# Storing the two halves of the latent heads' value product apart, and adding them when the outputs are loaded again

## The chip, the cores and the metric

The kernel runs on one core of one Trainium2 chip, in one launch. The metric is the device time of that launch in microseconds, as the median of repeated executions; less is better. Before the change the median of three executions is 1318.42 us (1316.21 to 1319.64). The core has five engines with an instruction queue each: TensorE (PE, with its weight loads as PEld), VectorE (DVE), ScalarE (ACT), GpSimd (POOL) and SyncE (SP). In this kernel SP issues every transfer, and the 16 DMA engines carry them out.

## What is computed

One layer of a streaming encoder on a sequence of 1024 tokens with 1024 channels, all in float32: a modulated norm, a mixer with two groups of eight attention heads, one output projection with a gated residual, and a gated MLP with a causal convolution. What matters here is the mixer's first group, the latent heads, and the projection behind both groups:

```
q, k, v from low-rank latents, 8 heads, q and k 96 wide, v 64 wide
o_mla = mla_attention(q, k, v)          # softmax(q k^T / sqrt(96)) v, chunk-causal
o_ca  = chunk_attention(cq, ck, cv, rel_bias[l])     # 8 heads, 9-chunk key band
mixed = jnp.dot(jnp.concatenate([o_mla, o_ca], axis=-1), w_out[l])
x = x + g_a[:, None, :] * mixed
```

The result must keep nearly float32 accuracy. TensorE's fast number formats don't have it in one operand, so the kernel splits operands into a high and a low half (hi, the rounded value, and lo, what is left) and adds the products of the halves. That is why one matrix product here is two or three matmuls.

## The kernel before

**Order of the work.** The kernel is written in a tile framework. Tiles are drawn from pools by tag with a number of buffers, and a tile whose buffer is still in use makes its first writer wait. A planner puts the instructions of each engine in order ahead of time, by priority and by its own forecast of times; each engine then runs its queue strictly in that order, waiting on semaphores. Where the program says issue_after, the planner must keep that order.

**Attention.** The work is cut into units: one head and one half g of the 1024 queries (512 queries). First come 16 units of the band heads, then 16 of the latent heads (two groups of four heads, each with g = 0 and 1). A unit has four tiles of 128 queries. For each tile, TensorE makes the scores (L807), DVE takes the minimum of the negated scores (L826), ACT the exponential with its sum (L833), DVE the reciprocal of the sum (L835, L836), POOL the high half of the scaled probabilities (hi, L73 from L852) and DVE the low half (L855), both in float16. SP then issues a transpose by DMA (L867) of each piece into PT tiles. Three tiles later TensorE multiplies the transposed probabilities by the values (L895). Beside this chain runs other work on the same engines: up-projections for later heads, and the projection of the band heads' outputs into part_d (f_oca, L710).

**The end of a unit.** The stationary operand of L895 is 128 columns wide: the 64 columns of the values' high half and the 64 of their low half. So the product in PSUM, pv, holds two partial results, in partitions 0 to 63 and 64 to 127, for 512 queries. For an even head ACT copies partitions 64 to 127 of pv, scaled, into partitions 0 to 63 of an SBUF tile named om (L904), and DVE scales the other half and adds it to the tile (L905); for an odd head the halves change places. SP stores the 64 rows to oT_d in DRAM (L909), which holds the outputs of all heads, transposed: 8 blocks of 128 rows with two heads each, by 1024 tokens. The om tile has one buffer, and pv has one. The store of the very last unit is held back (the list held, L907) and issued only after the first four loads of the next stage; that unit's tile is from another pool (tag R).

**The output projection.** For each of eight tiles of 128 tokens, o_load (L1066) reads the four latent blocks from oT_d into a tile ol of 128 by 512 (256 KB, in pieces of 512 B, as 128 tokens of a row are contiguous; L1069). ACT makes the high half oh (L77, called from L1070), POOL puts the low half back into ol (L84, from L1071). TensorE then does 24 matmuls of 512 columns for the tile (L1188 by way of L154 to L156), which take the three products hi*hi, hi*lo and lo*hi for four blocks and two column halves. DVE adds part_d's row (L1193), multiplies by the gate gabc (L1194) and adds x (L1195). SP stores the sum (L1196), ACT squares it (L1197), POOL and DVE norm it (L1202), and TensorE transposes it for the MLP (L1096).

The loads for this stage are o_load for tiles 0 to 3, then the held store, then gabc, and for each tile pa from part_d (L1169) and x (L1173, issued after the last of the first four o_loads). The weights of the MLP's first columns, wu, are loaded here as well (L1145), and split by ACT and POOL. ol and oh have four buffers each, so o_load of tile t + 4 follows TensorE's work on tile t.

Of the kernel before, what the change touches and what calls it, by code (L numbers as in the profile page):

```python
# [13 lines left out]
F32 = mybir.dt.float32  # L14
# [4 lines left out]
AF = mybir.ActivationFunctionType  # L19
# [3 lines left out]
MUL, ADD, SUB, MIN, MAX = ALU.mult, ALU.add, ALU.subtract, ALU.min, ALU.max  # L23

P = 128
D = 1024
S = 1024
NT = S // P
ND = D // P
# [35 lines left out]
def layer_kernel(ctx, tc, I, out):  # L65
    nc = tc.nc
    pe, act, dve, pool, sp = nc.tensor, nc.scalar, nc.vector, nc.gpsimd, nc.sync

    def f32(ap):
        return ap.bitcast(F32)  # L70
# [4 lines left out]
    def hi_of(eng, o, i):  # L75
        if eng == "a":
            act.activation(o, i, AF.Copy)  # L77
        elif eng == "p":
            pool.tensor_scalar(o, i, 1.0, 0.0, op0=MUL, op1=ADD)
        else:  # L80
            dve.tensor_copy(o, i)

    def lo_of(eng, o, i, hi):
        (pool if eng == "p" else dve).tensor_tensor(o, i, f32(hi), op=SUB)  # L84

    cst = ctx.enter_context(tc.tile_pool(name="cst", bufs=1))
    dram = ctx.enter_context(tc.tile_pool(name="dram", bufs=1, space=bass.MemoryType.DRAM))
    oT_d = dram.tile([ND, P, S], F32, name="oT_d")
    part_d = dram.tile([NT, P, D], F32, name="part_d")
    ga_d = dram.tile([P, D], F32, name="ga_d")  # L90
    x1_d = dram.tile([NT, P, D], F32, name="x1_d")
# [23 lines left out]
    anchor = {}  # L115
# [22 lines left out]
    def rtile(name, shape=(P, 512), dt=F32):  # L138
        return apg.tile(list(shape), dt, name=name, tag="R", bufs=4)
# [596 lines left out]
    def qk_page(src, name, rows, tag, bufs, gain):  # L736

        pt = page_psum(src, name, rows)
        if gain is None:
            hi, lo = q2(f"{name}h"), q2(f"{name}l")  # L740
            act.activation(hi[:rows], pt[:rows], AF.Copy)
            dve.tensor_tensor(lo[:rows], pt[:rows], f32(hi[:rows]), op=SUB)
            return hi, lo
        pg = at.tile([P, 2, 512], F32R, name=name, tag=tag, bufs=bufs)
        act.activation(pg[:rows, 0], pt[:rows], AF.Copy, scale=gain)
        dve.scalar_tensor_tensor(pg[:rows, 1], pt[:rows], gain, f32(pg[:rows, 0]), op0=MUL, op1=SUB)
        return pg
# [22 lines left out]
    class Unit:  # L770


        def __init__(u, nm, base, rows, pages, vst, g, band, bias, odd, dst_d, vs):
            u.nm, u.base, u.rows, u.pages, u.vst, u.g = nm, base, rows, pages, vst, g
            u.band, u.bias, u.odd, u.dst_d, u.vs = band, bias, odd, dst_d, vs
            u.pt = {}

        def scores(u, i):

# [92 lines left out]
        def values(u, i):  # L872

            if i % 4 == 1:
                u.pv = ps.tile([P, 512], F32, name=f"pv{u.nm}_{u.g}", tag="pv", bufs=1)
            c0 = (i % 4 - 1) * P
            todo = []
            for x in range(2):
                if (i - 1, x) not in u.pt:
                    continue  # L880
                tt, where = u.pt[i - 1, x]
                for j, at_ in where.items():
                    for h in range(2):
                        if len(at_) == 2:
                            b0, b1 = at_[0][h], at_[1][h]
                            todo.append((0, j, c0, 2 * P, tt[:, b0:b1 + 1:b1 - b0, :]))
                        else:
                            todo.append((1, j, c0 + at_[0][2] * P, P, tt[:, at_[0][h], :]))
            todo.sort(key=lambda v: v[0])
            with tc.high_priority(offset=OFF_V):  # L890
                for x, (_, j, c, w, mov) in enumerate(todo):
                    dst = u.pv[:, c:c + w]
                    if w > P:
                        dst = dst.rearrange("p (a b) -> p a b", a=2)
                    last = pe.matmul(dst, u.vst(j), mov, start=(x == 0), stop=(x == len(todo) - 1),  # L895
                                     skip_group_check=True)
                trail.append(last.ins)
                if i % 4 == 3:
                    final = u is units[-1]
                    dst = rtile(f"o{u.nm}_{u.g}") if final else \  # L900
                        at.tile([P, 512], F32, name=f"o{u.nm}_{u.g}", tag="o", bufs=1)
                    r0, r1 = (slice(64, 128), slice(0, 64)) if u.odd else (slice(0, 64), slice(64, 128))
                    inv = vscale[u.vs][1]
                    act.activation(dst[r0], u.pv[r1], AF.Copy, scale=inv[r1])  # L904
                    dve.scalar_tensor_tensor(dst[r0], u.pv[r0], inv[r0], dst[r0], op0=MUL, op1=ADD)  # L905
                    if final:
                        held.append(lambda: sp.dma_start(u.dst_d[r0, u.g * 512:(u.g + 1) * 512], dst[r0]))  # L907
                    else:
                        anchor["om"] = sp.dma_start(u.dst_d[r0, u.g * 512:(u.g + 1) * 512], dst[r0]).ins  # L909
            return 56 * sum(w // P for _, _, _, w, _ in todo)  # L910

    qlow = [at.tile([P, 512], F32R, name=f"qlow{n}") for n in range(3)]
# [6 lines left out]
    held = []  # L919
# [36 lines left out]
    def mla_unit(gr, hh, g):  # L956
        o = hh % 2

        def prep():
            q = qk_page(lambda j: mq[gr, (4 * g + j) // 2][:, j % 2, hh, :], f"mq{gr}{hh}_{g}", QK, "Q", 2, None)  # L960
            k = qk_page(lambda j: mk[gr, (4 * g + j) // 2][:, j % 2, hh, :], f"mk{gr}{hh}_{g}", QK, "K", 3, gk_m[:QK])
            pages[gr, hh, g] = (q, k)
        u = Unit(f"m{gr}{hh}", 0, QK,
                 lambda: (pages[gr, hh, g][0], [pages[gr, hh, i][1] for i in range(g + 1)]),
                 lambda j: mv[gr, j // 2][:, j % 2, hh].rearrange("p a b -> p (a b)"),
                 g, False, None, o, oT_d[2 * gr + hh // 2], ("m", gr))
        u.prep = prep
        u.need = [f"up{gr}"] if g == 0 else ["up1"]
        u.needv = []
        return u  # L970
# [55 lines left out]
    first = [anchor["pe"]]  # L1026
    units = [ca_unit(p, g, o) for p in range(4) for g in range(2) for o in range(2)]
    units += [mla_unit(gr, hh, g) for gr in range(2) for hh in range(4) for g in range(2)]
    ready = []
    tiles = [(u, i) for u in units for i in range(4 * u.g, 4 * u.g + 4)]  # L1030
    for n in range(len(tiles) + DEPTH):
        if n < len(tiles):
            u, i = tiles[n]
# [9 lines left out]
        if n >= DEPTH:  # L1043
            u, i = tiles[n - DEPTH]
# [18 lines left out]
    go = goo.__enter__()  # L1063
    oh, ol, ox = {}, {}, {}

    def o_load(t):  # L1066
        ol[t] = go.tile([P, 4, P], F32R, name=f"ol{t}", tag="ol", bufs=4)
        oh[t] = go.tile([P, 4, P], F32R, name=f"oh{t}", tag="oh", bufs=4)
        anchor["ol"] = sp.dma_start(f32(ol[t][:]), oT_d[0:4, :, t * P:(t + 1) * P].rearrange("k p t -> p k t")).ins  # L1069
        hi_of("a", oh[t][:], f32(ol[t][:]))  # L1070
        lo_of("p", ol[t][:], f32(ol[t][:]), oh[t][:])  # L1071

    for t in range(4):
        o_load(t)
# [569 lines left out]
def build(arrays):  # L1644
    nc = bacc.Bacc("TRN2", target_bir_lowering=False, num_devices=1, dynamic_dma_scratch_size=1024)
    I = {k: nc.dram_tensor(k, v.shape, mybir.dt.from_np(v.dtype), kind="ExternalInput").ap()
         for k, v in arrays.items()}
    out = nc.dram_tensor("out_0_dram", (S, D), F32, kind="ExternalOutput").ap()
    with tile.TileContext(nc, schedule_with_timeline_sim=True) as tc, ExitStack() as ctx:
        layer_kernel(ctx, tc, I, out)  # L1650
    return nc
# [8 lines left out]
```

## Time and profile before

| what | value |
|---|---|
| median of three executions | 1318.42 us |
| the profiled execution | 1320.49 us |
| its span, first to last instruction | 1318.7 us |
| mean granted TensorE clock | 0.964 of full |
| latent units: first and last copy of om on ACT | 399.2 and 599.6 us |
| output projection: first and last matmul of its tiles | 598.8 and 652.4 us |
| transfers issued | 190.83 MB in 223690 packets |
| loads of ol | 8 of 256.0 KB, median 9.3 us to landing |
| loads of x | 8 in this stage of 512.0 KB, median 9.4 us to landing |

The profile is one execution, taken by the hardware profiler. A group's row gives the line of the code, the engine, the operation, the tile written and the tiles read, the shape, how many there were, and min, median and max or the mean of one in ns. A row of the order of time begins with start and length in us; brackets behind it give the idle time of that engine just before and what ended it. A row of waits reads: who, for whom, us in total, times, longest. A row of stretches has the busy us of each engine with the number of instructions, then the granted clock, the share of the DMA engines that was busy, and GB/s. SPq is SP's queue: its rows are the issuing of transfers, and the transfer itself lands later.

### The profile page before, as it was taken

To read this page: it belongs to the slowest core of one execution; us is meant where nothing else is said; L and a number is where in the kernel's file an instruction comes from. 1 tells how busy PE (TensorE), PEld (TensorE's weight loads), DVE (VectorE), ACT (ScalarE), POOL (GpSimd) and SP (SyncE) were. 2 spreads that over 40 slices of the span, in tenths; PEclk is the share of its full clock that TensorE was granted. 3 is DMA by queue.
4 is the path that set the end of the run, shared out by engine and by line. 5 is a ranking of instruction groups with operands and counts; after the bars stand their busy time and mean duration, and the time that the engine had idled before them with its cause. 6 is when DMAs were issued, how large, how long until landed. Compare 5 with 4: busy or idle time off the path is not lost. (4 is left out here: it accounts for less than half of the span.)

```text
span 1318.7 us, 18701 instructions
## 1 busy us (share of the span) xinstructions
PE 1192.2 (90%) x6168; PEld 993.5 (75%) x6168; DVE 1080.2 (82%) x1864; ACT 627.3 (48%) x1148; POOL 597.4 (45%) x629
## 2 busy tenths in 40 slices
PE   4899889988768987868899999999999999999998
PEld 3789889878546766756777888888888886888886
DVE  6979988887589988874789888888889887687667
ACT  5455654455656454542375444443444444433331
POOL 5485773586687643454616444554444431000000
PEclk9999898989879899989999999999999999999999
DMA  8416768665233687789602334333343337943441
GB/s 326 144 55 153 170 146 187 157 161 119 48 85 62 148 165 155 146 173 300 265 17 84 125 104 136 112 114 125 93 131 106 128 104 245 394 145 109 128 160 64
DMA packets 223690, 190.83 MB, mean 145 GB/s; under 512 B 148709, under 2 KB 166373, under 8 KB 223593
## 3 DMA queue, kind: packets, MB, share of 16 engines
q1 hardware_dynamic: 223592, 189.64, 50.5%
q8 instruction: 48, 0.79, 0.2%
q14 instruction: 50, 0.40, 0.1%
HBM read 117.50 MB, written 37.49 MB: 118 GB/s over the span
## 5 line engine op out<-in xcount | busy, mean ns | idle before, releaser
L77 ACT ACTIVATE dnP<-dnr 128x1024 fp32r<-128x1024 f32 x73 | 77.5, 1064 | 116.1 <-PE dnA_P L1471 46.4
L1443 DVE TENSOR_TENSOR dnP<-dnr,dnP 128x1024 fp32r<-128x1024 f32 x72 | 88.7, 1236 | 51.8 <-ACT dnP L77 51.7
L73 POOL TENSOR_SCALAR hlm<-Pm,rim 128x512 f16<-128x512 f32 (+3 forms) x96 | 67.9, 716 | 66.7 <-issue 22.5
L84 POOL TENSOR_TENSOR wf<-wu,wf 128x512 fp32r<-128x512 f32 x22 | 38.6, 1752 | 116.6 <-ACT wf L77 116.6
L84 POOL TENSOR_TENSOR wb<-wu,wb 128x512 fp32r<-128x512 f32 x22 | 44.9, 2040 | 84.5 <-ACT wb L77 56.9
L1305 DVE SCALAR_TENSOR_TENSOR u<-c,cvp,u 128x1023 f32<-128x1023 f32 x44 | 55.8, 1310 | 27.6 <-ACT u L1304 24.8
L855 DVE SCALAR_TENSOR_TENSOR hlm<-Pm,rim,hlm 128x512 f16<-128x512 f32 (+3 forms) x96 | 68.7, 728 | 6.4 <-POOL hlm L73 6.2
L73 POOL TENSOR_SCALAR hlc<-Pc,ric 128x640 f16<-128x640 f32 (+2 forms) x64 | 49.7, 780 | 47.3 <-DVE ric L836 18.4
L833 ACT ACTIVATE Pc<-sc,mc 128x640 f32<-128x640 f32 (+2 forms) x64 | 42.3, 661 | 54.3 <-DVE mc L822 37.2
L833 ACT ACTIVATE Pm<-sm,mm 128x128 f32<-128x128 f32 (+3 forms) x64 | 47.2, 737 | 37.3 <-DVE mm L826 20.0
L895 PE MATMUL pvm<-PTm,vt 128*128 128x256 f16 (+1 forms) x320 | 43.6, 284 | 22.6 <-DMA PTm<-hlm 21.6
L1304 ACT ACTIVATE u<-c,cvp 128x1024 f32<-128x1024 f32 x44 | 52.4, 1238 | 23.6 <-DVE c L1403 16.7
L895 PEld LDWEIGHTS <-vt 128*128 128x128 f16 x320 | 31.3, 105 | 35.9 <-DMA PTm<-hlm 15.8
L855 DVE SCALAR_TENSOR_TENSOR hlc<-Pc,ric,hlc 128x640 f16<-128x640 f32 (+2 forms) x64 | 51.3, 806 | 8.4 <-POOL hlc L73 8.2
L77 ACT ACTIVATE wc<-ws 128x512 fp32r<-128x512 f32 x21 | 13.3, 632 | 93.1 <-DVE ws L1153 87.2
L154 PE MATMUL ipq<-wq_s,hT 128*128 128x256 f32 x192 | 56.4, 294 | 0.0
L1306 DVE SCALAR_TENSOR_TENSOR u<-c,cvp,u 128x1022 f32<-128x1022 f32 x44 | 55.5, 1301 | 0.0
L155 PE MATMUL ipq<-wq_s,hT 128*128 128x256 f32 x192 | 55.0, 287 | 0.0
L156 PE MATMUL ipq<-wq_s,hT 128*128 128x256 f32 x192 | 55.0, 287 | 0.0
L1470 PE MATMUL dnA_P<-dnP 128*128 128x512 f32 x132 | 51.3, 389 | 0.0
L1471 PE MATMUL dnA_P<-dnP 128*128 128x512 f32 x132 | 51.3, 389 | 0.0
L1469 PE MATMUL dnA_P<-dnP 128*128 128x512 f32 x132 | 51.2, 389 | 0.0
(441 smaller groups left out, 4420.5 us busy)
## 6 DMA issues: line engine op xcount, KB each, us to landing
wu<-w_up SPq DMA_DIRECT2D x44, 512.0 KB, 3.6
dnr<-g_d SPq DMA_DIRECT2D x73, 256.0 KB, 2.7
aw<-w_ada SPq DMA_DIRECT2D x48, 256.0 KB, 3.2
g_d<-u SPq DMA_DIRECT2D x22, 512.0 KB, 3.0
dnr<-w_down SPq DMA_DIRECT2D x44, 256.0 KB, 5.4
adaw<-w_ada_a SPq DMA_DIRECT2D x16, 512.0 KB, 6.2
x<-x SPq DMA_DIRECT2D x16, 512.0 KB, 9.4
g_d<-gs SPq DMA_DIRECT2D x22, 256.0 KB, 2.8
```

The source lines that it names most:

```text
L73: pool.tensor_scalar(o, i, s, 1.0, op0=MUL, op1=MUL)
L77: act.activation(o, i, AF.Copy)
L84: (pool if eng == "p" else dve).tensor_tensor(o, i, f32(hi), op=SUB)
L154: pe.matmul(pt, sh, mh, start=(start and i == 0), stop=False)
L155: pe.matmul(pt, sh, ml, start=False, stop=False)
L156: last = pe.matmul(pt, sl, mh, start=False, stop=(stop and i == n - 1))
L833: act.activation(pr[:, :n], sv, AF.Exp, bias=m[:], scale=-1.0, accum_out=rsum[:, 0:1])
L855: dve.scalar_tensor_tensor(hl[:, w:2 * w], pp, ri[:], hl[:, :w], op0=MUL, op1=SUB)
L895: last = pe.matmul(dst, u.vst(j), mov, start=(x == 0), stop=(x == len(todo) - 1), skip_group_check=True)
L1305: dve.scalar_tensor_tensor(u[:, 1:], c[:, :S - 1], cvp[:, cv + 1:cv + 2], u[:, 1:], op0=MUL, op1=ADD)
L1306: dve.scalar_tensor_tensor(u[:, 2:], c[:, :S - 2], cvp[:, cv:cv + 1], u[:, 2:], op0=MUL, op1=ADD)
L1443: r = f(*a, **k)
```

## The change

Only the latent units take part; they are marked by a second DRAM tensor, low_d. For them ACT copies all 128 partitions of pv, scaled, in one instruction, and DVE adds nothing. The tile then holds both partial results, and SP stores them in two transfers of 64 rows: the one in partitions 0 to 63 to oT_d, the one in 64 to 127 to a new tensor oL_d, at the same rows and columns. (Which of the two is the high half's product doesn't matter, as they are added.) In o_load a second tile, low, with three buffers, is loaded from oL_d in the same form; DVE adds ol and low into low, and the two halves are made from low. The anchor for issue_after is now the second load.

```
+    oL_d = dram.tile([ND // 2, P, S], F32, name="oL_d")
...
-                    act.activation(dst[r0], u.pv[r1], AF.Copy, scale=inv[r1])
-                    dve.scalar_tensor_tensor(dst[r0], u.pv[r0], inv[r0], dst[r0], op0=MUL, op1=ADD)
+                    cols = slice(u.g * 512, (u.g + 1) * 512)
+                    if u.low_d is not None:
+                        act.activation(dst[:], u.pv[:], AF.Copy, scale=inv)
+
+                        def store():
+                            sp.dma_start(u.dst_d[r0, cols], dst[0:64])
+                            return sp.dma_start(u.low_d[r0, cols], dst[64:128])
+                    else:
+                        act.activation(dst[r0], u.pv[r1], AF.Copy, scale=inv[r1])
+                        dve.scalar_tensor_tensor(dst[r0], u.pv[r0], inv[r0], dst[r0], op0=MUL, op1=ADD)
+
+                        def store():
+                            return sp.dma_start(u.dst_d[r0, cols], dst[r0])
                     if final:
-                        held.append(lambda: sp.dma_start(u.dst_d[r0, u.g * 512:(u.g + 1) * 512], dst[r0]))
+                        held.append(store)
                     else:
-                        anchor["om"] = sp.dma_start(u.dst_d[r0, u.g * 512:(u.g + 1) * 512], dst[r0]).ins
+                        anchor["om"] = store().ins
...
+        u.low_d = oL_d[2 * gr + hh // 2]
...
-        anchor["ol"] = sp.dma_start(f32(ol[t][:]), oT_d[0:4, :, t * P:(t + 1) * P].rearrange("k p t -> p k t")).ins
-        hi_of("a", oh[t][:], f32(ol[t][:]))
-        lo_of("p", ol[t][:], f32(ol[t][:]), oh[t][:])
+        low = go.tile([P, 4, P], F32, name=f"ow{t}", tag="ow", bufs=3)
+        sp.dma_start(f32(ol[t][:]), oT_d[0:4, :, t * P:(t + 1) * P].rearrange("k p t -> p k t"))
+        anchor["ol"] = sp.dma_start(low[:], oL_d[:, :, t * P:(t + 1) * P].rearrange("k p t -> p k t")).ins
+        dve.tensor_tensor(low[:], f32(ol[t][:]), low[:], op=ADD)
+        hi_of("a", oh[t][:], low[:])
+        lo_of("p", ol[t][:], low[:], oh[t][:])
```

More of the change, by code (lines that the diff above doesn't have):

```diff
@@ L776, in __init__ @@
             u.pt = {}
+            u.low_d = None
         def scores(u, i):
```

## The prediction

> **What bounds the kernel now.** I read the page's shares first, then tables of busy time by stretch around the two places that the change touches, then the waits, then the order of each queue there.
>
> ```profile
> PE 1192.2 (90%) x6168; PEld 993.5 (75%) x6168; DVE 1080.2 (82%) x1864; ACT 627.3 (48%) x1148; POOL 597.4 (45%) x629
> 460.00:575.00 115.00, 94.69 (x569) 75.31 (x568) 95.97 (x244) 62.27 (x131) 52.94 (x68) 1.00 0.78 157
> ...
> 595.00:605.00 10.00, 8.93 (x39) 6.58 (x39) 0.76 (x1) 3.21 (x5) 4.25 (x4) 0.83 0.98 281
> 605.00:608.00 3.00, 3.00 (x15) 2.49 (x14) 1.96 (x2) 0.00 (x0) 0.81 (x1) 1.00 0.93 361
> 608.00:611.00 3.00, 3.00 (x15) 2.50 (x14) 0.49 (x1) 0.00 (x0) 0.00 (x0) 1.00 0.10 39
> 611.00:615.00 4.00, 4.00 (x20) 3.30 (x19) 1.24 (x2) 0.00 (x0) 0.00 (x0) 1.00 0.95 333
> 615.00:645.00 30.00, 23.96 (x99) 18.92 (x98) 22.61 (x17) 11.41 (x20) 22.02 (x20) 0.89 1.02 391
> 645.00:652.00 7.00, 7.00 (x33) 5.74 (x32) 6.70 (x6) 1.92 (x3) 4.34 (x3) 1.00 0.24 100
> ```
>
> The columns after each stretch and its length are PE, PEld, DVE, ACT and POOL busy, the granted clock, the share of the DMA engines and GB/s. TensorE leads over the whole span, but the change sits in two stages with other limits. In steady latent attention (460 to 575) PE is busy 94.69 of 115 us and DVE 95.97: neither is full, both are near 83%, so what holds is a chain that goes through several engines. In the output projection (595 to 645) the DMA engines are full, at 0.93 to 1.02, except for one hole, 608 to 611 at 0.10.
>
> What TensorE waits for in attention, and the hole:
>
> ```profile
> PE pvm L895 <- DMA PTm<-hlm: 21.6, 15, 4.6
> ...
> SPq L1173 <- DMA oT_d<-om: 7.0, 1, 7.0
> ```
>
> The numbers are us in total, times, and the longest. In attention the transposed probabilities are late 15 times, and SP issues those. The hole is the last row: the x loads stand behind the landing of the last unit's store of om, for 7.0 us. What follows from it, row by row:
>
> ```profile
> 594.81 2.20 SPq L1069 DMA_DIRECT2D ol<-oT_d  x4
> ...
> 602.52 0.46 SPq L907 DMA_DIRECT2D oT_d<-om  x1
> 610.11 0.81 SPq L1173 DMA_DIRECT2D x<-x  x2
> 610.97 0.90 SPq L1145 DMA_DIRECT2D wu<-w_up  x2
> ...
> 613.47 0.38 SPq L1069 DMA_DIRECT2D ol<-oT_d  x1
> ...
> 619.02 1.29 POOL L84 TENSOR_TENSOR wa<-wu,wa 128x512 fp32r<-128x512 f32 x1
> ...
> 627.16 1.26 POOL L84 TENSOR_TENSOR ol<-ol,oh 128x512 fp32r<-128x512 f32 x1
> ...
> 628.48 0.79 PE L156 MATMUL op<-wo,ol 128*128 128x512 f32 x1 [4.93 <-POOL ol L84]
> ```
>
> The store is issued at 602.52 behind gabc and four pa loads and has landed by 610.11. Only then go x and the w_up tiles. Their splits keep POOL until the low half of output tile 4 at 627.16, and TensorE, 4.93 us idle, takes up tile 4 at 628.48. From there the four last output tiles run without a gap to 652. **The stage's end is set by when that store lands.**
>
> **The change part by part.** It touches the 16 latent units; the 16 band units keep their add. Durations are of the profiled execution, 1320.5 us with a span of 1318.7; that is 0.16% above the median of 1318.42. I add the sum to the median.
>
> ```profile
> L904 ACT ACTIVATE om<-pvm,vabm x16: 681/683/688, 399.2 to 599.6; 64x512 f32<-64x512 f32 x16
> L905 DVE SCALAR_TENSOR_TENSOR om<-pvm,vabm,om x16: 665/749/757, 400.9 to 600.3; 64x512 f32<-64x512 f32 x16
> L909 SPq DMA_DIRECT2D oT_d<-om x15: 452/581/608, 403.6 to 588.2; - x15
> ...
> L533 ACT ACTIVATE latT<-lt_ps,pk x6: 679/688/691, 305.0 to 341.7; 128x512 fp32r<-128x512 f32 x6
> ```
>
> Step 1, the copy. ACT reads 128 partitions instead of 64. The nearest row is L533, a scaled copy of 128x512 from PSUM, 688 ns against 683: nothing.
>
> Step 2, the adds removed from DVE in attention. 15 units by 0.74 us is 11.1 us before 600; the 16th stands in an idle stretch, and its store waited for SP until 602.52. How much of 11.1 carries is read from what follows each add. The four in 500 to 545, each with what ends the run of work after it:
>
> ```profile
> 508.16 0.76 DVE L905 SCALAR_TENSOR_TENSOR om<-pvm,vabm,om 64x512 f32<-64x512 f32 x1
> ...
> 511.22 0.11 DVE L825 MEMSET sm<- 64x64 f32 x1 [0.42 <-PE sm L807]
> ...
> 515.58 0.73 DVE L905 SCALAR_TENSOR_TENSOR om<-pvm,vabm,om 64x512 f32<-64x512 f32 x1
> ...
> 521.11 0.16 DVE L835 RECIPROCAL rim<-rsm 128x1 f32<-128x1 f32 x1 [0.48 <-ACT Pm L833]
> ...
> 532.99 0.73 DVE L905 SCALAR_TENSOR_TENSOR om<-pvm,vabm,om 64x512 f32<-64x512 f32 x1
> ...
> 535.51 0.11 DVE L825 MEMSET sm<- 64x64 f32 x1 [0.61 <-PE sm L807]
> ...
> 537.87 0.76 DVE L905 SCALAR_TENSOR_TENSOR om<-pvm,vabm,om 64x512 f32<-64x512 f32 x1
> ...
> 540.53 1.11 ACT L833 ACTIVATE Pm<-sm,mm 128x1024 f32<-128x1024 f32 x1 [1.09 <-DVE sm L825]
> ```
>
> After the adds at 508.16 and 532.99 DVE comes to wait for scores from TensorE (511.22 and 535.51): I count their gain as lost there. After 515.58 DVE works on until it waits for an exponential, which had waited for DVE's minimum; after 537.87 an exponential waits 1.09 us for DVE. These two carry. Half: **-5.5 us**, between 0 and -11.1.
>
> Step 3, the second store on SP. Each is one more issue of 0.58 us plus 0.1 between issues, 0.68, and behind it on SP stand the transposes that TensorE waits for.
>
> ```profile
> 453.39 0.59 SPq L909 DMA_DIRECT2D oT_d<-om  x1
> 454.09 3.83 SPq L867 DMA_TRANSPOSE PTm<-hlm  x3
> ...
> 567.45 0.59 SPq L909 DMA_DIRECT2D oT_d<-om  x1
> 568.14 0.53 SPq L723 DMA_DIRECT2D part_d<-co  x1
> 568.77 0.37 SPq L703 DMA_DIRECT2D wor<-w_out  x1
> 569.38 6.92 SPq L867 DMA_TRANSPOSE PTm<-hlm  x5
> ```
>
> Here everything up to the transposes follows back to back. That is so for 7 of the 15 stores (453, 463, 498, 540, 567, 584, 588); the other 8 have a pause of 0.8 us or more before the next transpose, which takes in 0.68. 7 by 0.68 is **+4.8**, between 0 and 10.2. The om tile has one buffer, so ACT also waits for both landings; but without the add the first store can go 0.75 earlier, and the pair ends where the one did. Attention together: -0.7.
>
> Step 4, the added loads at the stage's start. SP issues eight loads instead of four before the held stores (the fourth added one also waits for its buffer, freed by POOL's work on tile 0). TensorE's first tile starts later: one more load ahead, then an add on idle DVE; this delay, under 2 us, is covered by the 4.93 us gap before tile 4. What is not covered is the queue: 4 by 256 KB more go ahead of the held store, whose landing opens the hole's end. At the 281 GB/s of the stretch 595 to 605, in which such loads are moved, 1.05 MB takes 3.7 us; at the 391 of 615 to 645 it takes 2.7. I take **+3.7**, since the first row has these loads in it.
>
> That row is 281 GB/s at share 0.98 with pieces of 512 B, against 391 at 1.02 with longer ones. The Trainium skill, "Perfetto Trace Analysis", section "DMA Optimizations", says that transfers under 2 KB carry much overhead each; the trace agrees (281 against 391), and without that rule the sum would be 1.0 lower.
>
> Step 5, the second held store. One more issue of 0.46 and 128 KB at 361 GB/s, 0.36, partly beside one another: **+0.5**, from 0 to 0.8. The Trainium skill, "SBUF — State Buffer", section "Can I just issue two DMAs to hit both halves?", says that two such transfers of partition halves serialize; by its 196 GB/s for 64 partitions an estimate is 0.7, and the sum would be 0.2 higher; no run here shows such a pair yet.
>
> Step 6, the eight adds at load time.
>
> ```profile
> L1231 DVE TENSOR_TENSOR hv<-hv,hv 128x512 f32<-128x512 f32 x4 | 2.8, 689 | 1.0 <-ACT hv L1098 1.0
> ...
> 641.69 1.22 DVE L1193 TENSOR_TENSOR pa<-pa,op 128x1024 f32<-128x1024 f32 x1 [1.58 <-PE op L156]
> 652.84 1.22 DVE L1193 TENSOR_TENSOR pa<-pa,op 128x1024 f32<-128x1024 f32 x1 [1.04 <-PE op L156]
> ```
>
> 8 by 0.69 is 5.5 us of DVE, which idles 7.4 of 30 us in 615 to 645. The first seven are hidden there, behind POOL's chain (tile 4's high half is not what TensorE waited for). The last comes near 641.69, from where DVE runs nearly without pause to the end of tile 7: **+0.7**, from 0 to 5.5. The four later added loads, 3.7 us more of a full DMA, delay tiles 5 to 7, which have 1.3 us or more at TensorE, and move with it: nothing, up to 3.
>
> Sum: -5.5 + 4.8 + 3.7 + 0.5 + 0.7 = **+4.2 us**. Nothing later gives it back: TensorE is close to full from there on. 1318.4 + 4.2 = 1322.6.
>
> **The rivals.** (A) Faster: DVE alone holds attention. All 11.1 us carry, and the second stores cost nothing since SP was waiting for DVE. With steps 4 to 6 (+4.9) that is -6.2, 1312.2. For it: DVE has the highest busy time in 460 to 575. Against: TensorE's longest wait is for transposes. It decides from 4.9 us carried, and shows from 8.9. Chance 0.24.
>
> The landing of om's stores, for the next rival:
>
> ```profile
> DMA to landing us min/median/max: 2.4/2.5/7.6
> ```
>
> (B) No difference: the om pair, ready 0.75 us earlier without the add, is placed ahead of the pa loads by the planner, which orders SP by its own forecast. It then lands without the backlog (2.5 us, the median, where the last took 7.6), the 3 us hole closes, and steps 4 and 5 fall away. What is left is -5.5 + 4.8 + 0.7 = 0, 1318.4. Against it: the added loads hold SP longer. Chance 0.28.
>
> (C) Slower than forecast: SP holds attention. Every second store delays a transpose (10.2) and the removed adds buy nothing, since DVE waits for scores instead: +15.1, 1333.5. For it: 21.6 us of TensorE's waits; against: 8 of 15 stores have a pause behind them. That the change does not do what it says would be this case: the add gone, its time back as a wait. Chance 0.12.
>
> **How the numbers follow.** The forecast, slower by about 4, has 0.36. Faster by over 0.3% (4.0 us, about what a measurement of this kernel can tell from no change) is A, 0.24; within it is B, 0.28; slower is the forecast and C, 0.48. The range goes to just past A, 1311, and to C, 1334; the planner may also order the whole of attention anew, which can move it either way within these ends, so it is not narrower.
>
> **What would show it.** Step 2: 16 rows fewer on DVE, and the stretch from the first latent copy to the last not over 3 us shorter. Step 3: more waits of TensorE on the transposes than 21.6 us. Steps 4 and 5: the x loads issued later by about 4 us relative to the first output load, and TensorE's start on tile 4 with them. Step 6: a first tile later by under 2 us, without effect on tile 4. Wrong would be: x loads no later, or attention shorter by more than 5 us.

## The result and the profile after

The changed kernel takes 1336.16 us (median of four executions, 1329.13 to 1339.83), the kernel before 1317.73 beside it. The ratio is 1.012, 95% interval 1.0089 to 1.0151: slower by 15.8 us (11.7 to 19.9). That is less than the two medians' distance of 18.4 us; differences below go by the ratios. The forecast was slower by 4.2 and 1322.6, the range ended at 1334: **the sign was right, and the size was nearly four times what was forecast.** The median lies 2.2 us outside the range; 15.8 us more than the 1317.73 beside it would be 1333.5, at its very end.

The page after: the busy shares have hardly moved, and DVE has eight instructions fewer (sixteen adds gone, eight come).

```profile
PE 1199.0 (90%) x6168; PEld 996.6 (75%) x6168; DVE 1083.5 (81%) x1856; ACT 624.4 (47%) x1148; POOL 589.0 (44%) x629
```

The instructions on the tile om after, with min, median and max in ns, then the first and the last start in us, and the landing of its stores:

```profile
L908 ACT ACTIVATE om<-pvm,vabm x16: 670/687/692, 399.7 to 607.6; 128x512 f32<-128x512 f32 x16
L911 SPq DMA_DIRECT2D oT_d<-om x16: 454/540/686, 400.4 to 613.4; - x16
L912 SPq DMA_DIRECT2D oL_d<-om x16: 571/587/637, 400.9 to 614.2; - x16
...
DMA to landing us min/median/max: 2.2/2.4/8.7
```

The last copy of a latent unit comes at 607.6 instead of 599.6, with the first at 399.7 instead of 399.2. The same view of the output projection's tile op, before and then after:

```profile
L156 PE MATMUL op<-wo,ol x64: 388/389/794, 600.1 to 652.4; 128*128 128x512 f32 x64
```

```profile
L157 PE MATMUL op<-wo,ol x64: 388/389/796, 614.7 to 669.6; 128*128 128x512 f32 x64
```

So the span's 15.4 us (1334.1 against 1318.7) are +8.0 up to the last latent copy, +9.2 from there to the last output projection matmul (62.0 instead of 52.8), and -1.8 behind it. These are two places with two explanations.

**Attention.** The stretch from the seventh latent copy to the last, before and after; columns as in the prediction:

```profile
491.30:599.60 108.30, 85.42 (x494) 66.81 (x493) 85.44 (x213) 53.93 (x112) 47.29 (x61) 0.94 0.78 162
```

```profile
491.10:607.60 116.50, 91.77 (x504) 72.58 (x502) 81.00 (x202) 52.28 (x111) 49.51 (x63) 0.88 0.79 163
```

All 8.2 us are in here. DVE lost its eleven instructions and 4.4 us of work, as intended. TensorE has ten matmuls more in the stretch and is busy 6.35 us longer, at a granted clock of 0.88 instead of 0.94. Much of that is work which stood ahead of the stretch before: of the 192 matmuls on the tile oc (the band heads' projection, 512 columns each) 120 lie in it instead of 102, and keep TensorE 34.80 us instead of 27.54. The loss is read more safely from the first latent copy to the last, which holds all 192 both times, before and after:

```profile
399.20:599.60 200.40, 164.37 (x916) 128.87 (x915) 167.25 (x412) 106.51 (x231) 105.03 (x124) 0.93 0.71 147
```

```profile
399.70:607.60 207.90, 168.73 (x914) 132.54 (x913) 153.86 (x395) 102.92 (x228) 101.63 (x123) 0.90 0.72 149
```

These are 7.5 us more: TensorE is busy 4.4 us longer with two matmuls fewer, and idle 3.1 us longer. Its waits for transposed probabilities, which were to show that SP is the cause, are hardly more than the 21.6 us of before in the whole kernel, in fewer pieces:

```profile
PE pvm L897 <- DMA PTm<-hlm: 23.4, 10, 4.8
```

Between the seventh latent copy and the last alone they are no more than before; the view of waits of that stretch, before and after:

```profile
PE pvm L895 <- DMA PTm<-hlm: 17.7, 11, 4.6
```

```profile
PE pvm L897 <- DMA PTm<-hlm: 16.1, 5, 4.8
```

How waits and clock go together is seen in the order of time on TensorE after (sm are the scores):

```profile
493.10 0.50 PE L155 MATMUL oc<-wo,ch 128*128 128x512 f32 x1 [1.74 <-ACT ch L77]
...
496.07 0.80 PE L157 MATMUL oc<-wo,cl 128*128 128x512 f32 x1 [0.45 <-POOL cl L84]
496.66 0.63 PE L155 MATMUL oc<-wo,ch 128*128 128x512 f32 x1
...
501.50 0.40 PE L157 MATMUL oc<-wo,cl 128*128 128x512 f32 x1
...
514.46 1.39 PE L897 MATMUL pvm<-PTm,vt 128*128 128x256 f16 x8 [2.52 <-DMA PTm<-hlm]
...
516.14 2.06 PE L809 MATMUL sm<-mk,mq_1h 96*128 96x512 f32 x4
```

After idle times of 1.74 and 0.45 the oc matmuls take 0.63 instead of 0.40, and are back at 0.40 by 501.5. After the wait of 2.52 four score matmuls take 2.06, where the kernel before, after a wait of 0.99, has them in 1.08:

```profile
509.65 1.08 PE L807 MATMUL sm<-mk,mq_1h 96*128 96x512 f32 x4 [0.99 <-ACT Pm L833]
```

The oc matmuls, which in the kernel before stand in sixes between the other work and fill TensorE's waits, stand together here in one block at 496 to 503 and are missing at 512, where the wait is.

**The output projection.** Order of time after, all engines:

```profile
603.50 0.43 SPq L1084 DMA_DIRECT2D ol<-oT_d  x1
...
611.14 0.79 PE L155 MATMUL op<-wo,oh 128*128 128x512 f32 x1 [5.23 <-ACT oh L77]
...
612.67 0.73 SPq L1085 DMA_DIRECT2D ow<-oL_d  x1
...
613.44 0.69 SPq L911 DMA_DIRECT2D oT_d<-om  x1
...
614.17 0.64 SPq L912 DMA_DIRECT2D oL_d<-om  x1
...
623.05 0.92 SPq L1190 DMA_DIRECT2D x<-x  x2
...
640.80 0.51 POOL L120 TENSOR_SCALAR ss<-ss 128x1 f32<-128x1 f32 x1
641.40 1.41 POOL L121 TENSOR_TENSOR r<-ss,nhalf 128x1 f32<-128x1 f32 x1
642.78 1.35 POOL L84 TENSOR_TENSOR ol<-ow,oh 128x512 fp32r<-128x512 f32 x1
...
644.18 0.80 PE L157 MATMUL op<-wo,ol 128*128 128x512 f32 x1 [5.09 <-POOL ol L84]
```

The 9.2 us by their steps: from the last copy to the first load of outputs -4.1 instead of -4.8 (+0.7); to the x loads 19.55 instead of 15.30 (+4.25); to POOL's low half of tile 4 19.73 instead of 17.05 (+2.7); to TensorE's start on it +0.1; from there to the last matmul 25.4 instead of 23.9 (+1.5).

### The profile page after: what moved, and what is told of

Same layout as the page of the kernel before. It is cut to its first block, busy times and chain, and to the rows that moved or that the text cites. A ratio compares the mean times of both kernels' runs of the same rounds, so it can differ in the third digit from the quotient of the medians.

```text
span 1334.1 us, 18706 instructions
## 1 busy us (share of the span) xinstructions
PE 1199.0 (90%) x6168; PEld 996.6 (75%) x6168; DVE 1083.5 (81%) x1856; ACT 624.4 (47%) x1148; POOL 589.0 (44%) x629
## 4 chain that ended last, share of the span: by engine, by line
PE 52%; DVE 7%; DMA 7%; POOL 3%; issue 3%; ACT 2%; SPq 1%; POOLq 0%; DVEq 0%; ACTq 0%
PE p L1151 10%; PE p L1152 10%; PE p L1153 10%; PE dnA_P L1486 2%; PE dnA_P L1488 2%; PE dnA_P L1487 2%; DMA PTm<-hlm 2%; PE sm L809 2%; PE dnB_P L1488 1%; PE dnB_P L1487 1%; PE dnB_P L1486 1%; DMA x<-x 1%; DVE hlm L857 1%; DVE mm L828 1%; PE pvm L897 1%
## 5 line engine op out<-in xcount | busy, mean ns | idle before, releaser
L73 POOL TENSOR_SCALAR hlm<-Pm,rim 128x512 f16<-128x512 f32 (+3 forms) x96 | 63.9, 676 | 81.4 <-DVE rim L838 18.4
L1322 DVE SCALAR_TENSOR_TENSOR u<-c,cvp,u 128x1023 f32<-128x1023 f32 x44 | 61.4, 1435 | 27.5 <-ACT u L1321 27.5
L84 POOL TENSOR_TENSOR wb<-wu,wb 128x512 fp32r<-128x512 f32 x22 | 41.9, 1906 | 68.7 <-ACT wb L77 53.3
L73 POOL TENSOR_SCALAR hlc<-Pc,ric 128x640 f16<-128x640 f32 (+2 forms) x64 | 49.3, 773 | 47.7 <-DVE ric L838 17.7
L897 PE MATMUL pvm<-PTm,vt 128*128 128x256 f16 (+1 forms) x320 | 44.3, 289 | 23.4 <-DMA PTm<-hlm 23.4
L1323 DVE SCALAR_TENSOR_TENSOR u<-c,cvp,u 128x1022 f32<-128x1022 f32 x44 | 64.8, 1512 | 0.0
```

The source lines that it names most:

```text
L73: pool.tensor_scalar(o, i, s, 1.0, op0=MUL, op1=MUL)
```

## The experiments

Three theories were held against each other. **S**: each latent unit's second store on SP is what attention pays, by its bytes or by its place in SP's queue. **O**: it is the order that the planner makes for the edited program. **H**, for the output stage: the fourth added load waits for its buffer, and keeps back the held stores, the x loads, w_up, POOL and tile 4. The expectations spell the theories out again. The table has every kernel; the third column is the stretch from the seventh to the last latent copy, the fourth that from the last copy to the last output projection matmul, both in the profiled execution. The ratio is not the quotient of the two medians.

| kernel | median; ratio to before (95%) | attention, us | output stage, us |
|---|---|---|---|
| before | 1317.73 to 1319.83 in five series | 108.3 | 52.8 |
| changed | 1336.16; 1.012 (1.0089 to 1.0151) | 116.5 | 62.0 |
| e3_loads_only | 1322.77; 1.0046 (1.002 to 1.0071) | 106.4 | 58.7 |
| e1_no_add | 1322.02; 1.0021 (1.0001 to 1.0041) | 107.2 | 54.5 |
| e2_two_stores | 1321.45; 1.0015 (0.9991 to 1.004) | 114.3 | 49.5 |
| e13_one_store | 1321.57; 1.0025 (1.0004 to 1.0045) | 102.7 | 61.6 |
| e21_split_store | 1330.79; 1.0097 (1.0064 to 1.013) | 116.5 | 59.3 |
| e14_small_second_store | 1332.26; 1.0107 (1.0081 to 1.0132) | 113.7 | 63.6 |
| e19_second_store_act | 1326.91; 1.0052 (1.0037 to 1.0067) | 108.8 | 59.3 |
| e8_second_store_only | 1320.45; 1.0012 (0.9993 to 1.0031) | 107.8 | 52.9 |
| e4_last_tile | 1334.11; 1.0117 (1.0074 to 1.0159) | 116.5 | 58.4 |
| e15_held_store_first | 1341.22; 1.0171 (1.0135 to 1.0207) | 114.3 | 67.2 |
| e17_both_fixes | 1338.08; 1.0137 (1.01 to 1.0173) | 117.4 | 66.8 |
| e5_before_last_tile | 1313.69; 0.9962 (0.9947 to 0.9977) | 107.6 | 49.3 |

### The load side alone

Attention as before; each tile is loaded twice and added (in o_load, against the kernel before):

```
+        low = go.tile([P, 4, P], F32, name=f"ow{t}", tag="ow", bufs=3)
+        sp.dma_start(f32(ol[t][:]), oT_d[0:4, :, t * P:(t + 1) * P].rearrange("k p t -> p k t"))
+        anchor["ol"] = sp.dma_start(low[:], oT_d[0:4, :, t * P:(t + 1) * P].rearrange("k p t -> p k t")).ins
+        dve.tensor_tensor(low[:], f32(ol[t][:]), low[:], op=ADD)
...
```

> Load side alone: attention, its add and its one store as before; each output tile is loaded twice from the same tensor and added, so the latent outputs are doubled. My steps 4 to 6 gave 4.9 less 0.5 for the second held store: +4.4, 1322. The trace of the changed kernel shows the output stage (last copy of om to last output matmul) longer by 9.2, from 52.8 to 62.0: if all of that hangs on the load side, the stage is 61 to 62 here and the time 1326 to 1327; if part of it comes with the changed attention, it is less.

It is slower by 6.1 us (2.6 to 9.4), the stage by 5.9. Its order of time, SP and TensorE:

```profile
592.66 0.53 SPq L1070 DMA_DIRECT2D ol<-oT_d  x1
...
611.44 0.81 SPq L1176 DMA_DIRECT2D x<-x  x2
...
630.16 0.80 PE L156 MATMUL op<-wo,ol 128*128 128x512 f32 x1 [0.96 <-POOL ol L84]
```

The x loads go 18.8 us after the first load instead of 15.3, so four loads ahead of them cost 3.5, and tile 4 follows, 37.5 instead of 33.7. From tile 4 to the end of the stage it takes 24.8 instead of 23.9. Steps 4 and 6 of the forecast are this, and near its numbers.

### The attention side alone, with one store and with two

The copy of 128 rows without the add, loads as before; the first kernel stores 64 rows once, the second stores both halves:

```
-                    act.activation(dst[r0], u.pv[r1], AF.Copy, scale=inv[r1])
-                    dve.scalar_tensor_tensor(dst[r0], u.pv[r0], inv[r0], dst[r0], op0=MUL, op1=ADD)
+                        act.activation(dst[:], u.pv[:], AF.Copy, scale=inv)
...
+                            return sp.dma_start(u.dst_d[r0, cols], dst[0:64])
```

and in the second, instead of the last line,

```
+                            sp.dma_start(u.dst_d[r0, cols], dst[0:64])
+                            return sp.dma_start(u.low_d[r0, cols], dst[64:128])
```

> Attention side alone, without the second store: one copy of all 128 partitions, no add, one store of 64 rows; the load side is that of before. It leaves out the low half's products of the latent heads. Theory S (the second stores on SP's queue made attention 8 us longer): with them gone the last copy of om comes at or before 599.6 us, as before or up to 5.5 earlier, and the time is 1312 to 1318. Theory O (the planner put attention in another order once the add was gone, and TensorE runs at a lower granted clock in that order; the stores cost little): the last copy still comes 5 to 8 us late, 605 to 608, and the time is 1323 to 1326.

> As the attention side alone, but with both stores; the load side is that of before, so half of each sum is left out when the outputs are loaded. Theory S: the last copy of om at 607 to 608, as with the whole change, and 8 us or more later than with one store; time 1325 to 1328. Theory O: within 2 us of the kernel with one store in that copy, and the time higher by at most 2 (the second held store, 0.5 to 1).

The two times don't differ. Taking the add away gains nothing: 1.0021. The traces do differ, by stretches that cancel; first e1, then e2:

```profile
494.20:601.40 107.20, 85.73 (x488) 67.23 (x487) 80.79 (x207) 52.44 (x111) 45.47 (x61) 0.90 0.82 164
```

```profile
494.40:608.70 114.30, 88.99 (x504) 70.23 (x502) 81.24 (x202) 51.92 (x112) 49.19 (x63) 0.91 0.79 165
```

With two stores attention is 7 us longer, and the output stage 5 shorter (e2's profile is its slowest execution of ten, 5.2 us above its median, so its stretches are long ones): there the planner placed the held stores behind the first pa load instead of the fourth, and TensorE waits 1.06 us for tile 4 instead of 4.93. This is rival B's mechanism, at work. At this point S stood well.

### One store for both halves, and the same store cut in two

The whole change with one store of 128 rows into one array, and four loads of 64 partitions for a tile:

```
-                            sp.dma_start(u.dst_d[r0, cols], dst[0:64])
-                            return sp.dma_start(u.low_d[r0, cols], dst[64:128])
+                            return sp.dma_start(u.low_d[:, cols], dst[:])
...
```

> The whole change, but both halves of a unit leave in one store of 128 rows into one array, and each tile is put together from four loads of 64 partitions. Theory S (the second store of each unit makes attention longer): the last latent copy comes at 599 to 601 us as with one store, not at 607.6, and of the 9.2 us that the output stage lost at least 9.2 remain, since it has sixteen loads where the change has eight: 1327 to 1332 us. Theory O (the order that the planner makes once the add is gone is worse, whatever is stored): the last copy at 605 to 609 us and 1334 to 1340 us.

The last copy comes at 592.5, sooner than in any other kernel, and the time is 1321.57:

```profile
489.80:592.50 102.70, 83.18 (x490) 64.80 (x488) 79.07 (x202) 50.83 (x107) 46.15 (x60) 0.93 0.81 173
```

Then that store is cut in two and nothing else is edited:

```
-                            return sp.dma_start(u.low_d[:, cols], dst[:])
+                            sp.dma_start(u.low_d[0:64, cols], dst[0:64])
+                            return sp.dma_start(u.low_d[64:128, cols], dst[64:128])
```

> The kernel with one store of 128 rows per latent unit (1321.57 us), with that store cut into two of 64 rows into the same array, so that the same bytes leave in two stores, and nothing else edited. Theory S (a second store per unit is what the attention part pays, by the queue or by the order that follows from it): the last latent copy moves from 592.5 to 602 to 608 us and the time is 1330 to 1337 us. Rival (the single array and the four loads per tile are what made the one-store kernel quicker): 1319 to 1324 us, as with one store.

```profile
488.50:605.00 116.50, 89.88 (x504) 71.52 (x502) 80.28 (x202) 52.42 (x110) 47.13 (x63) 0.89 0.77 161
```

Fourteen us of attention, and 1.0097 instead of 1.0025, for a store cut in two. That looks like S, but the columns of counts show something else: the 504 matmuls of the changed kernel, exactly. Laid beside that kernel's by tile and shape, TensorE's queue here is the same for its first 3126 matmuls, into the output stage. So it is, up to the output stage at least, in e2, e4, e14, e15 and e17. The kernel with one store has another order from matmul 2436 on, at 454.7 us. Store and order had changed together, and both theories gave this result.

### The order kept, the bytes taken away

The changed kernel with second stores of 4 KB; the order of the engines is that of the changed kernel, but for two neighbours on DVE that change places:

```
-                            return sp.dma_start(u.low_d[r0, cols], dst[64:128])
+                            return sp.dma_start(u.low_d[r0, u.g * 512:u.g * 512 + 16], dst[64:128, :16])
...
-        anchor["ol"] = sp.dma_start(low[:], oL_d[:, :, t * P:(t + 1) * P].rearrange("k p t -> p k t")).ins
+        anchor["ol"] = sp.dma_start(low[:], oT_d[0:4, :, t * P:(t + 1) * P].rearrange("k p t -> p k t")).ins
```

> The whole change in the very order of the changed kernel on every engine, but each second store carries 64 rows of 16 columns, 4 KB in place of 128 KB, and the second load of each tile reads the first array again (the low half's products are left out). Theory S by bytes (the 2 MB of second stores slow the other transfers of attention): the last latent copy at 600 us or sooner, and 1327 us or less. Theory S by the queue (the issue of the second store stands between the transposes on SyncE's queue, whatever it carries) and theory O (the order that the planner makes for two stores is the loss): nothing changes, the last copy at 604 to 609 us and 1333 to 1340 us.

```profile
485.20:598.90 113.70, 91.87 (x504) 73.11 (x503) 80.28 (x202) 52.06 (x111) 49.01 (x63) 0.87 0.73 155
```

1.0107 against 1.012. The last copy itself came as early as S by bytes asked for, 598.9, but the time did not, and the trace shows why: this execution, the fastest of four, was ahead already at the seventh copy (485.2 against 491.1), and the stretch behind it is again long, 113.7, with 504 matmuls at a clock of 0.87. With the bytes as the cause the time should have fallen by 9 us or more; by the ratios it fell by 1.7 (the intervals overlap), so the bytes are not the main cause. The DMA rows say the same: a store of 4 KB lands hardly sooner than one of 128 KB.

```profile
oL_d<-om SPq DMA_DIRECT2D x16, 4.0 KB, 2.1
```

### The second store on another queue

```
-                            return sp.dma_start(u.low_d[r0, cols], dst[64:128])
+                            return act.dma_start(u.low_d[r0, cols], dst[64:128])
```

> The whole change, with the second store of each latent unit issued by ScalarE behind its own copy instead of by SyncE. Theory S by the queue (SyncE's queue with its transposes is what the second store delays): the last latent copy at 593 to 600 us, 1322 to 1329 us. Theory S by bytes: no gain, 604 us or later and 1333 us or more. Rival (ScalarE is delayed in place of SyncE, by its issues, and attention waits for ScalarE's copies instead): 600 to 606 us, 1330 us or more.

```profile
489.50:598.30 108.80, 87.46 (x496) 69.24 (x494) 79.21 (x207) 52.21 (x111) 45.55 (x61) 0.90 0.84 168
```

1.0052: the same work, bytes and number of stores as the changed kernel, some 9 us quicker, with attention as long as before. What is left, 6.9 us (4.9 to 8.8), is the output stage (+6.5). Here too the order had changed (from matmul 2249 on), so S by the queue and O both still stood.

### Two stores on SP, another order

The kernel before, add and loads kept, with each latent unit's rows stored a second time:

```
+                        if u.low_d is not None:
+                            last = sp.dma_start(u.low_d[r0, cols], dst[r0])
```

> The kernel before, add and loads as they were, with one thing added: each latent unit's 64 rows leave a second time, by a second store from SyncE into an array that nothing reads. Theory S (a second store on SyncE per latent unit costs attention some 7 us, whether or not the add is there): the last latent copy at 603 to 608 us, and 1324 to 1329 us against about 1319. Rival (it is the missing add that spoils the order, and the store costs only where the add is gone): the last copy at 596 to 601 us and 1317 to 1322 us.

```profile
492.10:599.90 107.80, 83.16 (x483) 64.56 (x482) 84.22 (x213) 53.76 (x112) 46.28 (x63) 0.92 0.84 171
```

1.0012, and attention as before: sixteen second stores on SP cost 1.6 us (-0.9 to 4.1) in this order, which is not clear of nothing. **As a price of the store by itself, S falls in both forms; O remains.** Seven kernels with the changed kernel's order of attention have 113.7 to 117.4 us there, with any store. Seven in five other orders have 102.7 to 108.8, with one store or two, with the add or without.

Two things limit this. The stretch doesn't hold the same work in both groups: 120 of the 192 oc matmuls in the first, 96 to 102 in the second. From the first latent copy to the last, with all 192 in every kernel, the first group takes 202.0 to 208.9 us (mean 206.2), the second 195.0 to 202.4 (199.1); the means are 7.1 us apart, and the ranges touch. And the first group is made up of exactly the kernels that have no add and two stores on SP, so a cost that arises only where the two meet can't be told from the order. If it came by late transposes, TensorE's waits for them should be longer there; between the seventh and the last copy they are 12.6 to 16.1 us in the first group and 9.7 to 17.7 in the second.

### The start of the output stage

Two edits to the changed kernel, alone and together: the last unit's tile is taken from the pool of the other units' outputs, so that the x loads don't wait for the held stores to land (e4, e17); and the held stores are let go after the last load from oT_d (e15, e17).

```
-                    dst = rtile(f"o{u.nm}_{u.g}") if final else \
-                        at.tile([P, 512], F32, name=f"o{u.nm}_{u.g}", tag="o", bufs=1)
+                    dst = at.tile([P, 512], F32, name=f"o{u.nm}_{u.g}", tag="o", bufs=1)     # e4, e17
...
-        sp.dma_start(f32(ol[t][:]), ...)
-        anchor["ol"] = sp.dma_start(low[:], ...).ins
+        anchor["ol"] = sp.dma_start(f32(ol[t][:]), ...).ins     # e15, e17
+        sp.dma_start(low[:], ...)
```

> The whole change, with the last unit's tile taken from the pool of the other units, so that the x loads don't stand behind the landing of its stores. If that landing sets the start on output tile 4 (my reading before), the x loads issue right behind the held stores at about 615 instead of 623, and the time falls by 4 to 8 us, to 1328 to 1332. Rival: DMA backlog and POOL's order set it, and the x loads that go earlier only lengthen the backlog for the second loads: the time stays within 2 us of 1336.

> The whole change, with the held stores let go after the last load of the first array instead of after the last load of the second, which waits for a buffer of three. Theory H (the missing fourth buffer keeps back the held stores, and with them the x loads, the w_up loads, GpSimd's splits and tile 4): the held stores issue some 4 us sooner after the first load of outputs (9.9 us in the changed kernel), the x loads with them (19.05), and the time is 1331 to 1334 us; the attention part is not touched, so the last latent copy stays at 606 to 609 us. Rival (tile 4 is late for another reason, GpSimd's own order): x loads sooner, tile 4 not, 1335 to 1337 us.

> As the one before it, and the last unit's outputs in the pool of the others besides, so that the x loads wait neither for the fourth buffer nor for the held stores. Theory H: the whole interaction of about 7 us goes, what is left is the longer attention and the four added loads, 1327 to 1330 us, and the stage from the last latent copy to the last output projection is 55 to 57 us instead of 62.0. Rival (GpSimd's order or the clock after the wait sets it): 1332 to 1335 us, as with the last tile alone (1334.1).

(The x loads' 19.05 us in the second text is 19.55 by the rows above.) The last tile alone shortens the stage to 58.4; tile 4 comes with a wait of 1.80 instead of 5.09:

```profile
639.66 0.53 PE L157 MATMUL op<-wo,ol 128*128 128x512 f32 x1 [1.80 <-POOL ol L84]
```

On the time this is not beyond the intervals. Letting the held stores go early does to the start of the chain what H says, but the kernel is not faster (e15, 1.0171 with an interval that overlaps the changed kernel's), and its stage is 5.2 us longer:

```profile
598.11 0.43 SPq L1084 DMA_DIRECT2D ol<-oT_d  x1
...
604.32 0.78 SPq L911 DMA_DIRECT2D oT_d<-om  x1
...
609.84 1.02 SPq L1190 DMA_DIRECT2D x<-x  x2
...
636.20 0.79 PE L157 MATMUL op<-wo,ol 128*128 128x512 f32 x1 [2.05 <-POOL ol L84]
...
657.34 1.74 DVE L1086 TENSOR_TENSOR ow<-ol,ow 128x512 f32<-128x512 f32 x1
...
659.86 0.79 PE L155 MATMUL op<-wo,oh 128*128 128x512 f32 x1 [5.35 <-ACT oh L77]
```

The x loads go 11.7 us after the first load instead of 19.55, tile 4 starts 38.1 after it instead of 40.7. But then TensorE waits 5.35 for tile 7: its added add stands in DVE's queue behind the sums of earlier tiles, which wait for TensorE's products. In e17 this wait is 5.72. H describes the first half of the stage only; by the trace the gain is given back in the second, by the order of DVE's queue.

### A version that beats both

The same edit of the last tile, in the kernel before:

> The kernel before, with one edit: the last unit's outputs go to the pool of the other attention outputs and not to a tile that the x loads take over, so that these loads need not wait for the held store to land. Theory H (what the output stage pays is the way held store, x loads, w_up loads, GpSimd, tile 4): the x loads start some 3 us sooner after the first load of outputs than the 15.3 us of before, tile 4 starts sooner by about 2 us, and the time is 1315 to 1317 us against about 1318. Rival (the x loads are not what tile 4 waits for): no difference, 1318 plus or minus 2.

```profile
593.08 2.21 SPq L1068 DMA_DIRECT2D ol<-oT_d  x4
...
601.08 0.42 SPq L1172 DMA_DIRECT2D x<-x  x1
```

```profile
623.52 0.50 PE L156 MATMUL op<-wo,ol 128*128 128x512 f32 x1 [3.09 <-POOL ol L84]
```

1313.69 us, 0.9962 (0.9947 to 0.9977), faster by 5.0 us. The x loads go 8.0 us after the first load instead of 15.3, the hole in the DMA traffic is shallower and shorter (a share of 0.26 from 599 to 601), tile 4 starts 30.4 after it instead of 33.7, and the stage is 3.5 shorter. The edit moved SP's order as well: the held store goes ahead of gabc and pa now, at 599.44.

## Why the prediction was right in its sign and wrong in its size

- **What bounds the stage: right.** That the output stage ends by when the held store lands is borne out from the other side: without that wait, and with the changed order on SP that came with it, it is 3.5 us shorter (e5).
- **Step 1: right.** The copy of 128 partitions takes 687 ns; 688 were forecast, 683 before.
- **Steps 2 and 3, "attention together -0.7": failed.** It was +8.0 in the profile. From the first latent copy to the last it is 7.5 us longer. Each term was priced as if the rest of the queue stayed where it was. Neither can be read from this kernel: without the add that part is 2.0 longer in one order (e1) and 5.4 shorter in another (e13), and the time is no shorter (1.0021 in e1); and the second store, put at +4.8, costs 1.6 (-0.9 to 4.1) in e8's order. What the runs showed in their place goes with the planner's new order of attention: 7.1 us more from the first latent copy to the last in the mean of seven profiles (206.2) than in the other seven (199.1). The prediction named this and gave it no term and no chance.
- **Steps 4 and 5: right.** The x loads are 4.25 us later behind the first load of outputs; +3.7 and +0.5 were forecast. With the loads alone it is 3.5 (e3): 1.05 MB at 300 GB/s, nearer to the 281 of the row chosen than to the 391. The Trainium skill, "SBUF — State Buffer", section "Can I just issue two DMAs to hit both halves?", puts such a pair at only 6% over a single transfer and says that the two serialize. No run here shows that for these stores: they land in 2.4 and 2.5 us, issued one after the other, one of 128 rows in 2.4 (e13) and one of 4 KB in 2.1 (e14), so their landing hardly depends on their size.
- **Step 6: right for the loads alone (+0.9 in e3, 0.7 forecast), +1.5 in the changed kernel.**
- **Missed in the output stage:** 2.7 us between the x loads and tile 4's low half. From POOL's first split of w_up to that low half it is 10.8 us instead of 8.1, with two pairs of small sums (L120, L121) between, where the kernel before and e3 have one. TensorE's first tile came later by 3.6 us and not by "under 2": 7.6 us after the first load instead of 4.0, 5.5 in e3; in the changed kernel two loads of w_out went directly ahead of that load.
- **The rivals.** A fell: DVE lost 4.4 us of work between the seventh copy and the last, and attention gained nothing. B's mechanism exists (e2), but not in the changed kernel, where the held stores went behind all four pa loads. C was nearest in size, 1333.5, and its reason is refuted: TensorE's waits for transposes are 23.4 us, not ten more, and second stores alone cost nothing that can be measured (e8).
- **Where luck comes in.** The sign follows from the load side alone: e3 is slower by 6.1 us. That the time comes so near the end of the range is luck, since that end was C's.

**What stays open.** Why the planner comes to this order when the add is gone and two stores are on SP isn't known. Whether the order would be as slow with the add in it, or with one store, wasn't tried; so that the order itself is the cause is argued from what the runs exclude, not shown. Of attention's 7.5 us between the first copy and the last, 4.4 are slower matmuls and 3.1 more idle time. That the slower clock follows from grouped waits is read from the order of time, not shown by an experiment: from 500 to 545 us the granted clock is 0.85 to 0.92 in the seven kernels of this order and 0.96 to 1.00 in the others, but from the first copy to the last it is 0.88 to 0.92 and 0.90 to 0.97.

## What to carry to other kernels

Where a planner orders the queues, an edit is worth its own cost plus the difference between two orders, and here the second, some 7 us going by the two groups, was larger than every term of the sum; a range must hold it. Before a cost is pinned on an operation, lay the queues of the kernels side by side: one run with the order kept and the cost taken away (e14) and one with the cost kept in another order (e8) took the blame off the store alone, which the runs with one edit each could not. And a profile that names a wait at the start of a stage is worth an edit of its own: freeing the tile that the x loads waited for was a gain of 5 us, though in the changed kernel the same edit gave no time that could be measured.

## What the runs showed of the hardware

- TensorE can slow down for a few microseconds amid short waits: in the changed kernel matmuls take 0.63 us instead of 0.40 after idle times of 1.74 and 0.45 us, at a granted clock of 0.59 from 493 to 500, and are back at 0.40 some 5 us later. The Trainium skill, "TensorE: Matmul & The Clock Gate", section "Part 1: The HAM clock gate", has the half clock come after an idle window of about 3.4 us; no idle time of that length stands there, so here the clock fell without one. Yet the kernel before had waits of up to 1.6 us in this part at a granted clock of 1.00; which waits lower it the runs don't tell.
- A store's landing hardly depends on its size here: 2.1 us for 4 KB, 2.4 for 128 KB, 2.4 for 256 KB (medians).
- Executions of one kernel spread widely: ten of e2 went from 1314.93 to 1326.67. The end of attention in a single profile moves by several us with the same order (598.9 to 608.7 in the changed kernel's).
